# Second FFN: the order of high and low products inside a unit of matmuls, from "weights' low parts last" to triples

## The chip, the core and the metric

The kernel runs on one core of one Trainium2 chip. The metric is the device time of one execution in microseconds (us), as the median over runs; smaller is better.

## What is computed

One layer of a hybrid diffusion backbone on 256 latent tokens and 256 context tokens of width 2048, all in float32: a half-step SwiGLU FFN, a token mixer (grouped-query attention beside a two-way mLSTM), a second half-step FFN on the latent tokens alone, and a final norm. The change touches the second FFN:

```python
def half_step_ffn(x, mod, i, g, w_up, w_down):
    h = adaln(x, g, mod, i)
    a, b = jnp.split(h @ w_up, 2, axis=-1)
    return x + 0.5 * mod[:, i + 2, None, :] * ((jax.nn.silu(a) * b) @ w_down)
...
    xl = half_step_ffn(xl, mod_l, 6, g_norm[l, 2], w_ffn2_up[l], w_ffn2_down[l])
return rms_norm(xl, g_final)
```

Here `x` is 256 x 2048, `w_up` 2048 x 11264 and `w_down` 5632 x 2048.

## The kernel before

**A product in three matmuls.** Each float32 operand is split in two parts that TensorE takes in its faster float32 form: a high part `hi` and the rest `lo`. A product is then high x high, low x high and high x low. The tokens' parts (`h2hi`, `h2lo`, the forms `n1f`, `s4f`, `s2f`, and the hidden values `hid2h`, `hid2l`) stay in SBUF and are the stationary operand (128 x 128); the weights are the moving one (128 x 512). In the names of the profile `mm<-hi,hid2h` is a matmul with the weights' high part moving and the hidden values' high part stationary; `mm<-lo,hid2h` has the weights' low part moving.

**A unit.** Weights arrive as tiles of 128 x 2048 (1 MB). `split` (line 116) makes two halves of 1024 columns from a tile: for each half ScalarE (ACT) writes `hi` (line 124), then VectorE (DVE) writes `lo` as tile minus `hi` (line 125). There are four buffers of `hi` and four of `lo`, which is two tiles' worth. The matmuls on one tile are a unit. `products_in_order` (line 150) lays a unit out: first, for every product, high x high and tokens' low x weights' high; at the unit's end all products of the weights' low part. `issue` (line 165) emits them.

**The second FFN** has 11 groups of 512 hidden columns. Groups 2 to 10 run as a `quad` (line 2092), which forms the group's up products (256 tokens x 2048 x 1024) from seven block products instead of eight. Its seven steps (a11, a12, n1, s4, s2, s3, a22; lines 2150 to 2158) have two units each, called q0 and q1 here, with 12 matmuls to a unit, and gather in the PSUM banks `X` and `Y`. Sums of weight tiles that the scheme needs are made in place: on the tiles `chain2c` and `chain2r` by DMAs that add while they land (`accum`, line 751, issued by GpSimd, POOL), and once per quad by VectorE (in step n1, 128 x 2048, line 2094). Three steps give such DMAs, two each, as soon as both halves of the tile are split: a11 (they are read in n1), s4 and s2 (those of s2 are read in a22). The other weights come by plain DMAs on SyncE's queue (SP).

**Down products** of earlier groups are woven in between: `block` (line 2196) is a unit of 24 matmuls, for two token halves t = 0, 1 with a PSUM bank each. In quads after the first there is one block behind each of the steps a12, n1, s2 and s3 (line 2280). `down_pair` (line 2219) gathers two groups in PSUM before VectorE adds the bank of each t to `acc2` (`acc<-acc,mm`, line 2233). Group 1's up products (`up`, line 2172, 24 matmuls a unit) are woven into the first quad. After the last quad `down` (line 2238) adds the gate and, by DMA, the residual (line 1048 is the gate's product), and `last2` (line 2297) ends with the norm.

**Order.** The kernel emits instructions in the order of these loops; a scheduler in the language then sets the order on each engine, and may move an instruction whose operand comes late, by its own estimate. At run time each engine goes through its list in that order and stands at the first one that waits.

Of the kernel before, what the change touches and what calls it, by code (L numbers as in the profile page):

```python
# [41 lines left out]
FB = 4  # L42
CB = 512
# [11 lines left out]
def tile_layer(ctx: ExitStack, tc: tile.TileContext, I: dict, out: bass.AP):  # L55
# [7 lines left out]
    ps = {"mm": banks.enter_context(pool(name="ps", bufs=6, space=PSUM)), "tr": banks.enter_context(pool(name="pt", bufs=2, space=PSUM))}  # L63
# [86 lines left out]
    def products_in_order(ps, weights_still=False):  # L150

        early, late = [], []
        for o, sh, sl, mh, ml, first, last in ps:
            early.append((o, sh, mh, first, False))
            if weights_still:
                early.append((o, sh, ml, False, False))
                late.append((o, sl, mh, False, last))
            else:  # L160
                early.append((o, sl, mh, False, False))
                late.append((o, sh, ml, False, last))
        return early + late

    def issue(ms, skip=False):
        for o, st_, mv, first, last in ms:
            tensor[0].matmul(o, st_, mv, start=first, stop=last, skip_group_check=skip)  # L167
# [1107 lines left out]
    with ExitStack() as mx:  # L1275
# [586 lines left out]
        for cb in range(NCB):  # L1862
            bs = []
# [86 lines left out]
    with f2x:  # L1950
# [141 lines left out]
        def quad(n):  # L2092

            add = lambda o, x, y: nc.vector.tensor_tensor(o, x, y, op=ALU.add)
            mul = lambda o, x, y: nc.vector.tensor_tensor(o, x, y, op=ALU.mult)
            B, g = {}, {}
            chain_, ra = sets[n % 2], sets[1 - n % 2]

            def p1():
                g["a"] = ca_tile()  # L2100
                nc.scalar.activation(g["a"], B["X"], AF.Copy)

            def c11():
                add(g["a"], B["Y"], g["a"])
                nc.scalar.activation(g["a"], g["a"], AF.Silu)

            def kept():
                g["y"] = f2b.tile([P, CB], F32, tag="cy", name="cy", bufs=1)
                nc.scalar.activation(g["y"], B["Y"], AF.Copy)

            def p35():
                g["b"] = ca_tile()
                nc.scalar.activation(g["b"], B["Y"], AF.Copy)

            def c12():
                add(g["b"], B["X"], g["b"])
                mul(g["a"], g["a"], g["b"])
                turn.append((clock[0] + 2, n, 0, g["a"], -1.0))

            def c22():  # L2120
                assert (n, 0) in done
                add(g["y"], B["X"], g["y"])
                g["a"] = ca_tile()
                nc.scalar.activation(g["a"], B["X"], AF.Copy)

            def c21():
                add(g["a"], B["Y"], g["a"])
                nc.scalar.activation(g["a"], g["a"], AF.Silu)
                mul(g["a"], g["a"], g["y"])
                turn.append((clock[0] + 4, n, 1, g["a"], -1.0))  # L2130

            def chained(ab, c):
                return lambda q: accum(chain_[q], part(n, ab, c + q))

            def next_first(q):
                if n + 1 in QUADS:
                    nc.sync.dma_start(ra[q], part(n + 1, 0, q))

            def next_third(q):
                if n + 1 in QUADS:  # L2140
                    nc.sync.dma_start(chain_[q], part(n + 1, 1, 2 + q))

            def plain(q):
                r = raw_tile()
                nc.sync.dma_start(r, part(n, 0, 2 + q))
                return r

            held = lambda q: chain_[q]
            third = lambda q: ra[q]
            order = (  # L2150
                (a11, held, "X", True, chained(1, 0), p1),
                (a12, plain, "Y", True, None, c11),
                (n1, held, "Y", True, lambda q: add(chain_[q], chain_[q], ra[q]), kept),
                (s4, third, "Y", False, lambda q: accum(ra[q], part(n, 1, q)), p35),
                (s2, held, "X", False, chained(0, 2), c12),
                (s3, third, "X", False, next_first, c22),
                (a22, held, "Y", True, next_third, c21),
            )
            for m, (a, src, dst, fresh, then, use) in enumerate(order):
                for q in range(2):  # L2160
                    if q == 0 and fresh:
                        B[dst] = psx.tile([P, 512], F32, tag=dst, name=dst)
                    wt = split(src(q))
                    if then:
                        then(q)
                    ks = [(j, 4 * q + j) for j in range(4)]
                    issue(products_in_order([(B[dst], a[0][:, k, :], a[1][:, k, :], *wt(slice(j * CB, (j + 1) * CB)), fresh and k == 0, k == 7) for j, k in ks]), True)
                    if q:
                        use()
                    yield  # L2170

        def up(n):

            sab = []
            for ab in range(2):
                bs = [bank() for _ in range(2)]
                for u in range(4):
                    wt = load_split(part(n, ab, u))
                    ps = []
                    for j in range(4):  # L2180
                        k = 4 * u + j
                        for t in range(2):
                            tt = slice(t * P, (t + 1) * P)
                            ps.append((bs[t], h2hi[:, k, tt], h2lo[:, k, tt], *wt(slice(j * CB, (j + 1) * CB)), k == 0, k == KT - 1))
                    issue(products_in_order(ps))
                    if u == 3:
                        for t in range(2):
                            if ab:
                                nc.vector.tensor_tensor(sab[t], sab[t], bs[t], op=ALU.mult)
                                turn.append((clock[0] + 2, n, t, sab[t], 1.0))  # L2190
                            else:
                                sab.append(acc2[:, t, :CB])
                                nc.scalar.activation(sab[t], bs[t], AF.Silu)
                    yield

        def block(n, wt, ts=(0, 1), bs=None, first=True, last=True):

            bs = bs or [bank() for _ in ts]
            ps = []
            for j in range(FB):  # L2200
                for t, b in zip(ts, bs):
                    tt = slice(t * P, (t + 1) * P)
                    ps.append((b, hids[n][0][:, j, tt], hids[n][1][:, j, tt], *wt(slice(j * CB, (j + 1) * CB)), first and j == 0, last and j == FB - 1))
            issue(products_in_order(ps))
            return bs

        late = {}
# [241 lines left out]
```

## Time and profile before

| | |
|---|---|
| median of 3 runs | 2619.69 us (2619.2 to 2623.19) |
| the profiled execution | 2623.62 us, of which the span from first to last instruction is 2621.9 us |
| granted TensorE clock | 0.996 |
| TensorE busy | 2577.2 us (98%) |
| VectorE busy | 2167.5 us (83%) |
| ScalarE busy | 1420.9 us (54%) |
| second FFN's quads and what follows | from about 1953 us to the end |

Times in the views are in us from the start of the span. In a timeline a row has start, duration, engine, line, operation, output<-inputs, and how many instructions it merges; in square brackets is the idle time of the engine before it and what ended it. The ends of matmuls are modelled: they are issued every 0.227 us, while a row gives one 0.39 us, so the last 0.16 us of each lies beside the next. A group row gives busy time and mean ns, then idle time before.

### The profile page before, as it was taken

How to read it: one execution, taken by the hardware profiler on the slowest of the kernel's cores; microseconds unless marked ns; L12 is line 12 of the kernel's file. 1: busy time of each engine (PE TensorE's matmuls, PEld its weight loads, DVE VectorE, ACT ScalarE, POOL GpSimd, SP SyncE). 2: the span in 40 equal slices, each digit the busy share in tenths (PEclk: the TensorE clock that was granted, in tenths of full speed). 3: DMA queues.
4: the chain of work that ended last, by engine and by line, in shares of the span. 5: the costliest groups of instructions: out<-in, count | busy, mean ns of one | idle time of the engine just before them, and what ended most of it. 6: DMA issues, size and time to landing. Idle time of an engine off the chain costs nothing. (4 is left out here: it accounts for less than half of the span.)

```text
span 2621.9 us, 34118 instructions
## 1 busy us (share of the span) xinstructions
PE 2577.2 (98%) x12646; PEld 2139.4 (82%) x12646; DVE 2167.5 (83%) x2842; ACT 1420.9 (54%) x1876; POOL 216.4 (8%) x271
## 2 busy tenths in 40 slices
PE   8999999999999999999999999999999999999998
PEld 5788888888888888888889889888898877777776
DVE  7788888878888788888787889788898888888888
ACT  5454444454444465444454467567576656666664
POOL 0000010100010100000110000110000000000001
PEclk9999999999999999999999999999999999999999
DMA  9989999999999988889976877677678889998996
GB/s 401 350 210 269 277 270 284 256 272 285 275 268 284 263 242 235 226 218 231 228 233 261 306 275 246 230 262 277 235 277 236 253 249 259 261 263 259 262 266 192
DMA packets 127654, 684.71 MB, mean 261 GB/s; under 512 B 14200, under 2 KB 16760, under 8 KB 64896
## 3 DMA queue, kind: packets, MB, share of 16 engines
q1 hardware_dynamic: 98112, 490.63, 49.9%
q0 software_dynamic: 29376, 191.90, 37.1%
q8 instruction: 99, 1.62, 0.2%
q14 instruction: 67, 0.55, 0.1%
HBM read 664.59 MB, written 17.89 MB: 260 GB/s over the span
## 5 line engine op out<-in xcount | busy, mean ns | idle before, releaser
L125 DVE TENSOR_TENSOR lo<-raw,hi 128x1024 fp32r<-128x1024 f32 (+2 forms) x476 | 561.9, 1205 | 152.6 <-ACT hi L124 107.3
L124 ACT ACTIVATE hi<-raw 128x1024 fp32r<-128x1024 f32 (+2 forms) x488 | 492.1, 1036 | 345.0 <-PE mm L167 214.7
L167 PE MATMUL mm<-hi,hhi 128*128 128x512 f32 (+3 forms) x1024 | 392.1, 385 | 0.0
L167 PE MATMUL mm<-hi,hlo 128*128 128x512 f32 (+3 forms) x1024 | 386.0, 379 | 0.0
L124 ACT ACTIVATE hi<-chain 128x1024 fp32r<-128x1024 f32 x240 | 247.1, 1055 | 222.7 <-PE mm L167 109.4
L125 DVE TENSOR_TENSOR lo<-chain,hi 128x1024 fp32r<-128x1024 f32 x240 | 288.0, 1221 | 88.2 <-ACT hi L124 80.4
L167 PE MATMUL mm<-lo,hhi 128*128 128x512 f32 (+3 forms) x1024 | 253.4, 378 | 0.0
L228 DVE SCALAR_TENSOR_TENSOR junk<-sraw,cBh 128x1024 fp8e5<-128x1024 f32 x192 | 234.5, 1221 | 15.5 <-DMA sraw<-in_w_mt 13.3
L167 PEld LDWEIGHTS mm<-hi,hhi 128*128 128x128 f32 x1024 | 193.5, 189 | 31.5
L167 PEld LDWEIGHTS mm<-hi,hlo 128*128 128x128 f32 x1024 | 193.5, 189 | 31.1
L167 PEld LDWEIGHTS mm<-lo,hhi 128*128 128x128 f32 x1024 | 187.0, 188 | 33.1
L125 DVE TENSOR_TENSOR lo<-chain2c,hi 128x1024 fp32r<-128x1024 f32 x112 | 133.9, 1222 | 48.0 <-ACT hi L124 39.8
L125 DVE TENSOR_TENSOR lo<-chain2r,hi 128x1024 fp32r<-128x1024 f32 x104 | 124.1, 1222 | 48.1 <-ACT hi L124 40.4
L124 ACT ACTIVATE hi<-chain2c 128x1024 fp32r<-128x1024 f32 x112 | 113.0, 1052 | 87.8 <-DMA chain2c<-in_w_up2b 51.2
L124 ACT ACTIVATE hi<-chain2r 128x1024 fp32r<-128x1024 f32 x104 | 104.9, 1052 | 84.9 <-DMA chain2r<-in_w_up2b 37.1
L167 PE MATMUL mm<-hi,hid2h 128*128 128x512 f32 x352 | 137.2, 390 | 0.0
L167 PE MATMUL mm<-hi,hid2l 128*128 128x512 f32 x352 | 137.1, 390 | 0.0
L228 DVE SCALAR_TENSOR_TENSOR sr<-sr,cBl 128x1024 f32<-128x1024 f32 x85 | 102.7, 1218 | 14.8 <-DMA sr<-in_w_mt 14.7
L751 POOL DMA_DIRECT2D chain<-in_w_up1b x60 | 53.0, 884 | 728.0 <-DVE lo L125 700.7
L167 PE MATMUL mm<-lo,hid2h 128*128 128x512 f32 x352 | 87.6, 389 | 0.0
L167 PE MATMUL mm<-hhi,hi 128*128 128x512 f32 (+1 forms) x256 | 83.7, 346 | 0.0
L167 PE MATMUL mm<-hlo,hi 128*128 128x512 f32 (+1 forms) x256 | 81.2, 336 | 0.0
(512 smaller groups left out, 5609.0 us busy)
## 6 DMA issues: line engine op xcount, KB each, us to landing
raw<-in_w_dn SPq DMA_DIRECT2D x70, 1024.0 KB, 10.5
chain<-in_w_up1b POOLq DMA_DIRECT2D x60, 1024.0 KB, 9.8
sraw<-in_w_mt SPq DMA_DIRECT2D x96, 512.0 KB, 7.8
sr<-in_w_mt SPq DMA_DIRECT2D x82, 512.0 KB, 5.6
raw<-in_w_up1b SPq DMA_DIRECT2D x40, 1024.0 KB, 7.7
mraw<-in_w_m SPq DMA_DIRECT2D x32, 1024.0 KB, 7.7
chain<-in_w_dn POOLq DMA_DIRECT2D x30, 1024.0 KB, 9.3
chain2c<-in_w_up2b POOLq DMA_DIRECT2D x28, 1024.0 KB, 12.2
```

The source lines that it names most:

```text
L124: scalar[0].activation(hi, src, AF.Copy)
L125: vector[0].tensor_tensor(lo, src, hi.bitcast(F32), op=ALU.subtract)
L167: tensor[0].matmul(o, st_, mv, start=first, stop=last, skip_group_check=skip)
L228: ins = nc.vector.scalar_tensor_tensor(junk() if junk else raw, raw, 1.0, cB[s], op0=ALU.mult, op1=ALU.mult, accum_out=mT[:, i, s, kt, h : ...
L751: accum = lambda dst, src: nc.gpsimd.dma_start(dst, src, accum_op=ALU.add)
```

## The change

All units of the second FFN's quads, of `up` and of `block` are laid out in triples: for each product in turn high x high, high x weights' low, tokens' low x high. So the second matmul of a unit reads the weights' low part of the first half. In `block` the loop over token halves is now the outer one, so that t = 0's bank is complete after the first half of the unit. The first FFN and the mixer are as before. Three lines are new above, so later lines have numbers three higher.

```diff
+    def products_by_triple(ps):
+        return [m for o, sh, sl, mh, ml, first, last in ps for m in ((o, sh, mh, first, False), (o, sh, ml, False, False), (o, sl, mh, False, last))]
...
-                    issue(products_in_order([(B[dst], a[0][:, k, :], a[1][:, k, :], *wt(slice(j * CB, (j + 1) * CB)), fresh and k == 0, k == 7) for j, k in ks]), True)
+                    issue(products_by_triple([(B[dst], a[0][:, k, :], a[1][:, k, :], *wt(slice(j * CB, (j + 1) * CB)), fresh and k == 0, k == 7) for j, k in ks]), True)
...
-                    issue(products_in_order(ps))
+                    issue(products_by_triple(ps))
...
-            for j in range(FB):
-                for t, b in zip(ts, bs):
+            for t, b in zip(ts, bs):
+                for j in range(FB):
...
-            issue(products_in_order(ps))
+            issue(products_by_triple(ps))
```

The number of instructions is the same on every engine, and the orders on POOL and SP are the same. On TensorE the block behind step n1, in a quad of the middle of the second FFN, stood so before (its last high products and its low ones; `hi_17056` and `lo_17057` belong to the first half of the tile, `hi_17060` and `lo_17061` to the second, and `mm_17052`, `mm_17053` are the banks of t = 0 and 1):

```order
L167 MATMUL mm_17053<-hi_17060,hid2h_16591 128x512
L167 MATMUL mm_17053<-hi_17060,hid2l_16592 128x512
L167 MATMUL mm_17052<-lo_17057,hid2h_16591 128x512
L167 MATMUL mm_17053<-lo_17057,hid2h_16591 128x512
L167 MATMUL mm_17052<-lo_17057,hid2h_16591 128x512
L167 MATMUL mm_17053<-lo_17057,hid2h_16591 128x512
L167 MATMUL mm_17052<-lo_17061,hid2h_16591 128x512
```

The sixteen high products came first, and the second half's low part was read by the 21st matmul of the unit.

Now such a block begins as follows (`hi_18484`, `lo_18485` are the first half, `hi_18488`, `lo_18489` the second):

```order
L170 MATMUL mm_18480<-hi_18484,hid2h_17212 128x512
L170 MATMUL mm_18480<-lo_18485,hid2h_17212 128x512
L170 MATMUL mm_18480<-hi_18484,hid2l_17213 128x512
L170 MATMUL mm_18480<-hi_18484,hid2h_17212 128x512
L170 MATMUL mm_18480<-lo_18485,hid2h_17212 128x512
L170 MATMUL mm_18480<-hi_18484,hid2l_17213 128x512
L170 MATMUL mm_18480<-hi_18488,hid2h_17212 128x512
L170 MATMUL mm_18481<-hi_18484,hid2h_17212 128x512
L170 MATMUL mm_18481<-lo_18485,hid2h_17212 128x512
L170 MATMUL mm_18481<-hi_18484,hid2l_17213 128x512
L170 MATMUL mm_18481<-hi_18484,hid2h_17212 128x512
L170 MATMUL mm_18480<-lo_18489,hid2h_17212 128x512
```

The second matmul reads the first half's low part, and the scheduler has put four matmuls of t = 1 ahead of the first that reads the second half's low part: it is the 12th here, and the 8th in the units of the quads and nearly all other blocks.

On VectorE, around step n1 of such a quad (`chain2c` holds n1's two tiles, `raw` is the tile of the block behind it), the order before was:

```order
L125 TENSOR_TENSOR lo<-chain2c_16106,hi 128x1024
L2094 TENSOR_TENSOR chain2c_16106<-chain2c_16106,chain2r_16108 128x2048
L125 TENSOR_TENSOR lo<-chain2c_16107,hi 128x1024
L2233 TENSOR_TENSOR acc_16105<-acc_16105,mm 128x512 x2
L125 TENSOR_TENSOR lo<-chain2c_16107,hi 128x1024
L125 TENSOR_TENSOR lo<-raw,hi 128x1024
L2094 TENSOR_TENSOR chain2c_16107<-chain2c_16107,chain2r_16109 128x2048
L125 TENSOR_TENSOR lo<-raw,hi 128x1024
L125 TENSOR_TENSOR lo<-chain2r_16108,hi 128x1024 x2
```

and it is now:

```order
L125 TENSOR_TENSOR lo<-chain2c_16106,hi 128x1024
L2236 TENSOR_TENSOR acc_16105<-acc_16105,mm 128x512
L2097 TENSOR_TENSOR chain2c_16106<-chain2c_16106,chain2r_16108 128x2048
L2236 TENSOR_TENSOR acc_16105<-acc_16105,mm 128x512
L125 TENSOR_TENSOR lo<-chain2c_16107,hi 128x1024 x2
L125 TENSOR_TENSOR lo<-raw,hi 128x1024
L2097 TENSOR_TENSOR chain2c_16107<-chain2c_16107,chain2r_16109 128x2048
L125 TENSOR_TENSOR lo<-raw,hi 128x1024
L125 TENSOR_TENSOR lo<-chain2r_16108,hi 128x1024 x2
```

Both additions to `acc2` of the block before n1 have moved from between the two splits of n1's q1 tile to ahead of them.

Around step a22, before (`chain2r` holds a22's tiles):

```order
L125 TENSOR_TENSOR lo<-chain2r_16108,hi 128x1024
L125 TENSOR_TENSOR lo<-chain2r_16109,hi 128x1024
L2233 TENSOR_TENSOR acc_16105<-acc_16105,mm 128x512 x2
L125 TENSOR_TENSOR lo<-chain2r_16109,hi 128x1024
L125 TENSOR_TENSOR lo<-chain2c_16106,hi 128x1024 x2
```

and now:

```order
L125 TENSOR_TENSOR lo<-chain2r_16108,hi 128x1024
L2236 TENSOR_TENSOR acc_16105<-acc_16105,mm 128x512
L125 TENSOR_TENSOR lo<-chain2r_16109,hi 128x1024
L2236 TENSOR_TENSOR acc_16105<-acc_16105,mm 128x512
L125 TENSOR_TENSOR lo<-chain2r_16109,hi 128x1024
L125 TENSOR_TENSOR lo<-chain2c_16106,hi 128x1024 x2
```

One of the two additions has moved ahead of the first split of a22's q1 tile; the other still stands between the two.

## Prediction

> **What bounds the kernel now.** The page first: TensorE is busy nearly all the time.
>
> ```profile
> PE 2577.2 (98%) x12646; PEld 2139.4 (82%) x12646; DVE 2167.5 (83%) x2842; ACT 1420.9 (54%) x1876; POOL 216.4 (8%) x271
> ```
>
> An average can hide a stage, so next the stretches of 200 us (core time, then PE, PEld, DVE, ACT, POOL busy, granted clock, DMA share, GB/s), one from the first FFN and one from the second.
>
> ```profile
> 400.00:600.00 200.00, 200.00 (x901) 165.49 (x900) 159.12 (x201) 94.02 (x112) 19.41 (x22) 1.00 0.97 270
> 2200.00:2400.00 200.00, 191.48 (x843) 154.93 (x843) 165.68 (x155) 123.10 (x136) 15.67 (x18) 1.00 0.88 253
> ```
>
> The first FFN leaves TensorE no gap. The second does, at full clock, so something else paces it. Its quads repeat; three stretches cut at the ends of a22 show how long one takes.
>
> ```profile
> 2111.23:2177.25 66.02, 62.15 (x273) 49.91 (x272) 53.22 (x51) 39.76 (x45) 5.22 (x6) 1.00 0.88 255
> ...
> 2499.73:2561.49 61.76, 61.35 (x274) 50.20 (x272) 53.19 (x51) 39.77 (x45) 5.23 (x6) 1.00 0.87 241
> 2111.23:2561.49 450.26, 432.61 (x1906) 350.04 (x1904) 372.57 (x351) 278.92 (x309) 36.57 (x42) 1.00 0.89 257
> ```
>
> Seven quads take 450.26 us: 66.02 for the first, 61.76 for the last, and (450.26 - 66.02 - 61.76) / 5 = 64.50 for each of the five between. The last has no next quad to fetch for, and TensorE is busy in 61.35 of its 61.76 us. So TensorE's own work is at most 61.4 us a quad and the other five have about 3 us more. What are they waits for? The list of TensorE's waits in the second FFN (us in total, times, longest):
>
> ```profile
> PE Y L167 <- DVE lo L125: 12.5, 14, 1.0
> PE Y L167 <- ACT hi L124: 7.2, 8, 1.4
> ```
>
> TensorE waits only at units of `Y`, for splits: the places are q1 of n1 and q1 of a22, whose tiles come by adding DMAs. ScalarE's timeline has the starts of the splits when such tiles have landed (a22, n1, the next a22), and POOL's has the first adding DMA that is given after each.
>
> ```profile
> 2236.42 2.01 ACT L124 ACTIVATE hi<-chain2r 128x1024 fp32r<-128x1024 f32 x2 [3.89 <-PE Y L167]
> ...
> 2259.84 2.01 ACT L124 ACTIVATE hi<-chain2c 128x1024 fp32r<-128x1024 f32 x2 [3.22 <-DMA chain2c<-in_w_up2b]
> ...
> 2300.75 2.01 ACT L124 ACTIVATE hi<-chain2c 128x1024 fp32r<-128x1024 f32 x2 [3.91 <-PE Y L167]
> ```
>
> ```profile
> 2243.74 0.86 POOL L751 DMA_DIRECT2D chain2c<-in_w_up2b  x1 [27.88 <-DVE lo L125]
> ...
> 2271.64 0.88 POOL L751 DMA_DIRECT2D chain2r<-in_w_up2b  x1 [24.18 <-DVE lo L125]
> ```
>
> This is a loop: landing for a22 at 2236.42, 7.32 us until POOL gives the next DMA, 16.10 until the tile for n1 is in, 11.80 until the next DMA, 29.11 until a22's tile. Together 64.33: the quad's length. DMAs take 45.2 us of it, and the reaction to a landing, on ScalarE and VectorE, 19.1. VectorE's timeline at n1 shows what the 11.80 consist of:
>
> ```profile
> 2260.93 1.23 DVE L125 TENSOR_TENSOR lo<-chain2c,hi 128x1024 fp32r<-128x1024 f32 x1 [1.52 <-ACT hi L124]
> 2262.08 1.28 DVE L2233 TENSOR_TENSOR acc<-acc,mm 128x512 f32<-128x512 f32 x2
> 2263.27 1.22 DVE L125 TENSOR_TENSOR lo<-chain2c,hi 128x1024 fp32r<-128x1024 f32 x1
> 2264.41 1.22 DVE L125 TENSOR_TENSOR lo<-raw,hi 128x1024 fp32r<-128x1024 f32 x1
> 2265.54 2.29 DVE L2094 TENSOR_TENSOR chain2c<-chain2c,chain2r 128x2048 f32<-128x2048 f32 x1
> 2267.74 1.22 DVE L125 TENSOR_TENSOR lo<-raw,hi 128x1024 fp32r<-128x1024 f32 x1
> 2268.88 4.63 DVE L125 TENSOR_TENSOR lo<-chain2r,hi 128x1024 fp32r<-128x1024 f32 x4
> ```
>
> VectorE runs without a gap from 2260.93: split, two additions to `acc2`, split, split, weight sum, split, then s4's two splits, after which POOL can give s4's DMA.
>
> **The change, part by part.** *The matmuls themselves.* Same number, same form. TensorE's rows at n1:
>
> ```profile
> 2261.28 1.98 PE L167 MATMUL Y<-hi,n1f 128*128 128x512 f32 x8
> 2263.09 0.61 PE L167 MATMUL Y<-lo,n1f 128*128 128x512 f32 x2
> 2264.55 0.73 PE L167 MATMUL Y<-lo,n1f 128*128 128x512 f32 x2 [0.84 <-DVE lo L125]
> 2265.12 0.39 PE L167 MATMUL mm<-hi,hid2h 128*128 128x512 f32 x1
> ...
> 2270.57 1.98 PE L167 MATMUL Y<-hi,s4f 128*128 128x512 f32 x8
> ```
>
> Eight take 1.81 us, 0.227 each, and the block of 24 from 2265.12 to 2270.57 takes 5.45, high or low alike. New order within a bank: 0.
>
> *VectorE's order at n1.* Both additions move ahead of the tile's first split. Before it VectorE stands idle for 1.52 us, and the block that they add ended before n1, so there they cost nothing; behind it they took 2263.27 - 2262.08 = 1.19. The reaction becomes 11.80 - 1.19 = 10.61. If that cover were gone they would cost 1.19 again.
>
> *VectorE's order at a22.*
>
> ```profile
> 2237.50 1.23 DVE L125 TENSOR_TENSOR lo<-chain2r,hi 128x1024 fp32r<-128x1024 f32 x1 [4.48 <-ACT hi L124]
> 2238.65 1.28 DVE L2233 TENSOR_TENSOR acc<-acc,mm 128x512 f32<-128x512 f32 x2
> ```
>
> One of the two additions leaves the way: half of 1.19, 0.60 (here 4.48 us idle cover it).
>
> Whether 0.60 reaches the landing depends on the DMAs' load (last but one column):
>
> ```profile
> 2266.00:2268.00 2.00, 2.00 (x10) 1.65 (x10) 2.00 (x2) 0.99 (x2) 0.00 (x0) 1.00 0.00 0
> 2268.00:2270.00 2.00, 2.00 (x11) 1.65 (x10) 2.00 (x2) 1.15 (x2) 0.00 (x0) 1.00 0.10 16
> ...
> 2301.00:2308.00 7.00, 5.30 (x22) 3.85 (x22) 6.16 (x7) 6.41 (x7) 0.00 (x0) 1.00 0.97 377
> 2308.00:2317.00 9.00, 9.00 (x44) 7.42 (x43) 9.00 (x10) 6.69 (x10) 1.76 (x2) 1.00 0.99 229
> ```
>
> During the reaction at n1 the DMAs stand still, so 1.19 us less of it is 1.19 us less of quad. At a22 they are full (0.97, 0.99) with plain loads, and an earlier adding DMA only takes its share from those. Of the 0.60 I count 0.2, between 0 and 0.6. So a paced quad goes from 64.50 to 63.1 (-1.4), with 62.7 and 63.3 as ends. The Trainium skill, "DMA: Bandwidth & Descriptors", section "Issuing engines are not separate DMA queues", says that transfers from all issuing engines run on the same 16 DMA engines and interleave. By that rule alone the 0.60 would bring nothing, and a quad would take 63.3; the rows 0.97 and 0.99 agree.
>
> *TensorE's new waits.* It now needs the first half's low part at its second matmul. From n1's landing (2259.84 = 0), with 1.14 a split (2263.27 to 2264.41) and 2.20 for the sum (2265.54 to 2267.74): low parts of q1 at 2.2 and 3.4, of the block at 4.5 and 7.8. TensorE starts q1 at 1.44, goes on at 2.3, and 11 matmuls later has finished at 4.8; before at 5.28. The block's 12th matmul is due at 4.8 + 11 x 0.227 = 7.3 and waits until 7.9: 0.6. The block ends at 10.85, before at 10.73. At a22 q1 it has 2.2 us to wait for the low part after the landing instead of 1.1, but the second half is there 0.6 earlier: 0 to +0.4. Added to 61.4, TensorE's own quad is at most 62.4, below 63.1, so these waits lie in time in which it would wait for a tile anyway. Where no DMA paces, they show: I count 0.5 for each of the first two quads, 1.0 in all (0 to 3), and -0.3 for the last quad, whose n1 and a22 lose an addition's wait (0 to -0.6).
>
> *Buffers.* The first half's high part is free after 6 matmuls instead of 4, the second after 12 instead of 8: 0.45 and 0.9 us later. At s4 that gives its second high part 4.8 + 0.2 + 0.6 (a copy from `Y` now stands ahead of it on ScalarE) + 0.95 (half of the 2.01 rows) after the landing, 6.6; VectorE comes to it at about 9. Covered: 0.
>
> *The end.* VectorE's rows after the last block's weights have come:
>
> ```profile
> 2593.09 1.28 DVE L2246 TENSOR_TENSOR acc<-acc,mm 128x512 f32<-128x512 f32 x2
> 2594.29 1.29 DVE L1048 SCALAR_TENSOR_TENSOR acc<-acc,g 128x512 f32<-128x512 f32 x2
> 2595.49 3.49 DVE L125 TENSOR_TENSOR lo<-raw,hi 128x1024 fp32r<-128x1024 f32 x3
> ```
>
> Four instructions stand between two splits there; in the new order one addition of the four comes earlier, into VectorE's idle time: -0.6 (0 to -1.5).
>
> Sum: +1.0, six paced quads x -1.4 = -8.4, -0.3, -0.6: **-8.3 us**. The profiled execution took 2623.62, of which 2621.9 is span; it would take 2615.3. It lies 3.9 above the median of 2619.69, and I take the same difference from that: **2611.4**.
>
> **The rivals.**
>
> *More: TensorE alone paces.* If the accumulating DMAs also run faster because plain loads fall later, a quad comes down to TensorE's own 61.4 to 62.4, say 62.0: 6 x -2.5 - 0.9 + 1.0 = -14.9, 2604.8. For it: DMA share 0.89 leaves the DMAs some 7 us idle in a quad. Against: the 29.11 us stage has been full.
>
> *No change: the DMAs give nothing back.* The landing for a22 comes when four adding DMAs and the plain loads are through; if the plain loads take the 1.19 us, the quads stay at 64.5 and only +1.0 - 0.3 - 0.6 is left: 2619.8. For it: the shares of 0.97 and 0.99; against: 0.00 and 0.10 in the reaction.
>
> *Slower: the low part's wait is not hidden.* At both landings of a quad TensorE stands before its second matmul until VectorE's split is done, 1.1 us later than now, and holds everything behind it; finishing a unit after that takes 11 matmuls where now 2 or 4 are left. If VectorE does not come to the splits earlier (because the additions, now ahead of them in its order, wait for the block's second bank) each landing costs 0.7 and the block 0.6: 2.0 a quad, 7 x 2.0 + 1.0 = +15, 2634.7. It decides when the block before n1 ends so late that the second addition, 0.6 us, and a split, 1.14, are not done within n1 q0's 12 matmuls, 2.72 us: a margin of 0.9 now. The first FFN's down products already go in triples at 200.00 of 200.00 busy, which speaks against it. The Trainium skill, "TensorE: Matmul & The Clock Gate", Part 2, says that matmuls stay in program order and only weight loads are pulled ahead. By it a late low part stops the whole queue, which is this rival; the trace agrees, as the 0.84 above stopped the block behind it.
>
> **How the numbers follow.** A measurement of this kernel tells about 0.2%, 5.2 us, from no change. Forecast 0.45, more 0.12, no change 0.25, slower 0.18. Of the forecast's 0.45 a part (terms at their weak ends) falls inside 5.2 us: faster 0.53, same 0.29, slower 0.18. The range takes in the first three with their ends and the lighter part of the slower case: 2603 to 2626.
>
> **What would show it.** Right: quads of 63.1 in the cut stretches; first adding DMA 10.6 after n1's landing and 6.7 after a22's; TensorE's waits moved from n1 and a22 to the block behind n1, some 0.6 each. Wrong: quads still at 64.5 although the reaction is shorter (DMAs), or above it with longer waits for `lo` (slower), or additions on VectorE that wait for `mm` ahead of the splits.

## The result, and the profile after

The changed kernel takes 2609.86 us (median of 4 runs, 2605.14 to 2611.2), the kernel before beside it 2621.07 (4 runs, 2619.2 to 2623.19): a ratio of 0.9953, with a 95% interval of 0.9937 to 0.9969. That is 11.2 us less; 8.3 were forecast. The profiled execution took 2609.54 us, of which the span is 2607.8.

The page's line of engines hardly moved, TensorE's 2577.2 us became 2575.1:

```profile
PE 2575.1 (99%) x12646; PEld 2138.1 (82%) x12646; DVE 2172.8 (83%) x2842; ACT 1435.6 (55%) x1876; POOL 216.3 (8%) x271
```

The stretches cut at the ends of a22 show the quads: first, third, fourth and fifth, then all seven in one (columns as in the prediction).

```profile
2108.39:2171.16 62.77, 62.02 (x274) 50.04 (x272) 53.78 (x51) 41.37 (x44) 5.22 (x6) 1.00 0.93 269
...
2234.66:2300.56 65.90, 62.56 (x274) 50.02 (x272) 53.80 (x51) 41.13 (x44) 5.21 (x6) 1.00 0.89 255
2300.56:2362.34 61.78, 61.49 (x274) 50.19 (x272) 54.63 (x51) 41.74 (x44) 5.21 (x6) 1.00 0.92 265
2362.34:2423.81 61.47, 61.15 (x273) 50.20 (x272) 53.86 (x51) 41.57 (x44) 5.24 (x6) 1.00 0.92 273
...
2108.39:2548.71 440.32, 432.62 (x1906) 350.84 (x1905) 377.89 (x352) 290.24 (x308) 36.55 (x42) 1.00 0.91 265
```

Seven quads take 440.32 us where they took 450.26: 62.90 each on average, not 64.32. They are no longer alike: some run at 61.5 with TensorE busy nearly throughout, one takes 65.90. Between the two spans (2621.9 and 2607.8, 14.1 apart) the seven quads account for 9.9, the time up to the first cut (2111.23 and 2108.39) for 2.8, and the rest behind the last for 1.3.

TensorE's waits in the second FFN (us in total, times, longest) fell from 12.5 and 7.2 to:

```profile
PE Y L170 <- DVE lo L125: 3.6, 6, 0.8
PE Y L170 <- ACT hi L124: 1.9, 3, 1.1
PE mm L170 <- DVE lo L125: 1.7, 6, 0.3
```

The wait at `mm` is new, six times. The two reactions of the loop are read as before: ScalarE's splits of the tiles for a22, n1 and the next a22, which have just landed, and POOL's first adding DMA behind each.

```profile
2229.27 2.01 ACT L124 ACTIVATE hi<-chain2r 128x1024 fp32r<-128x1024 f32 x2 [3.84 <-DMA chain2r<-in_w_up2b]
...
2254.34 2.00 ACT L124 ACTIVATE hi<-chain2c 128x1024 fp32r<-128x1024 f32 x2 [3.81 <-DMA chain2c<-in_w_up2b]
...
2295.20 2.01 ACT L124 ACTIVATE hi<-chain2c 128x1024 fp32r<-128x1024 f32 x2 [3.97 <-DMA chain2c<-in_w_up2b]
```

```profile
2236.00 0.86 POOL L754 DMA_DIRECT2D chain2c<-in_w_up2b  x1 [26.97 <-DVE lo L125]
...
2264.93 0.88 POOL L754 DMA_DIRECT2D chain2r<-in_w_up2b  x1 [25.20 <-DVE lo L125]
...
2301.92 0.88 POOL L754 DMA_DIRECT2D chain2r<-in_w_up2b  x1 [26.81 <-DVE lo L125]
```

So 6.73 us at a22 (2229.27 to 2236.00), 18.34 until n1's tile is in, 10.59 at n1 (2254.34 to 2264.93), and 30.27 for the four DMAs. The reactions were 7.32 and 11.80. These rows are from the slowest of the seven quads: its stage of 18.34 stands out, the other six took 15.3 to 17.0 there. VectorE's timeline at this n1 shows the difference:

```profile
2253.71 0.68 DVE L2236 TENSOR_TENSOR acc<-acc,mm 128x512 f32<-128x512 f32 x1
2255.42 2.36 DVE L125 TENSOR_TENSOR lo<-chain2c,hi 128x1024 fp32r<-128x1024 f32 x2 [1.03 <-ACT hi L124]
2257.70 1.22 DVE L125 TENSOR_TENSOR lo<-raw,hi 128x1024 fp32r<-128x1024 f32 x1
2258.84 2.28 DVE L2097 TENSOR_TENSOR chain2c<-chain2c,chain2r 128x2048 f32<-128x2048 f32 x1
2261.04 1.22 DVE L125 TENSOR_TENSOR lo<-raw,hi 128x1024 fp32r<-128x1024 f32 x1
2262.17 2.35 DVE L125 TENSOR_TENSOR lo<-chain2r,hi 128x1024 fp32r<-128x1024 f32 x2
```

Both additions are through before VectorE's idle 1.03 us ends, and from there to s4's second split nothing is left but splits and the weight sum.

### The profile page after: what moved, and what is told of

Read it like the earlier page. It is cut to its first block, busy times and chain, and to the rows that moved or that the text cites. A ratio compares the mean times of both kernels' runs of the same rounds, so it can differ in the third digit from the quotient of the medians.

```text
span 2607.8 us, 33942 instructions
## 1 busy us (share of the span) xinstructions
PE 2575.1 (99%) x12646; PEld 2138.1 (82%) x12646; DVE 2172.8 (83%) x2842; ACT 1435.6 (55%) x1876; POOL 216.3 (8%) x271
## 4 chain that ended last, share of the span: by engine, by line
PE 78%; DMA 10%; DVE 6%; issue 3%; ACT 1%; POOL 0%; SPq 0%; POOLq 0%; ACTq 0%; DVEq 0%
PE mm L170 48%; PE mm L147 4%; PE mm L148 4%; PE mm L146 4%; DMA chain2c<-in_w_up2b 4%; PE Y L170 4%; DMA chain2r<-in_w_up2b 3%; DVE lo L125 3%; PE X L170 2%; PE mm L83 2%; PE tr L147 2%; PE tr L148 2%; PE tr L146 2%; DMA mraw<-in_w_m 1%; ACT hi L124 1%
## 5 line engine op out<-in xcount | busy, mean ns | idle before, releaser
L124 ACT ACTIVATE hi<-raw 128x1024 fp32r<-128x1024 f32 (+2 forms) x488 | 497.7, 1038 | 358.5 <-PE mm L170 208.7
L170 PE MATMUL mm<-lo,hid2h 128*128 128x512 f32 x352 | 137.8, 392 | 1.7 <-DVE lo L125 1.7
L170 PEld LDWEIGHTS mm<-lo,hid2h 128*128 128x128 f32 x352 | 66.1, 188 | 18.4 <-DVE lo L125 5.0
```

Source lines behind the costliest of these rows:

```text
L124: scalar[0].activation(hi, src, AF.Copy)
```

## Experiments

**The theory**: the gain is the 1.19 us (n1) and 0.60 us (a22) that two VectorE additions no longer take between a landing and the next adding DMA. **Rival one**: TensorE gains from the triples. **Rival two**: buffers freed later spread the plain loads, so the adding DMAs land sooner. The table holds every run. The reactions are from the start of ScalarE's split to POOL's next adding DMA, as above; where engine order alone sets them they repeat to 0.02 us from quad to quad. In late_add_pin, late_sum_pin and late_sum_pb the split at a22 starts when TensorE frees a buffer, in nearly every quad, and the tile has landed before that. The quads are the seven, from one profiled execution each. The ratio is to the kernel before, timed on the same chip.

| kernel | at n1 | at a22 | quads, mean | median | ratio (95%) |
|---|---|---|---|---|---|
| before | 11.80 | 7.32 | 64.32 | 2621.07 | |
| before, again | 11.80 | 7.32 | 64.00 | 2616.07 (one run) | |
| the whole change | 10.61 | 6.73 | 62.90 | 2609.86 | 0.9953 (0.9937-0.9969) |
| block_only | 10.61 | 6.73 | 63.80 | 2612.69 | 0.9961 (0.9947-0.9974) |
| quads_only | 11.80 | 7.33 | 64.43 | 2618.15 | 0.9993 (0.9977-1.0008) |
| per_bank | 10.61 | 6.73 | 62.65 | 2610.07 | 0.9952 (0.9935-0.9969) |
| late_add_pin | 11.93 | 7.3-7.6 | 65.22 | 2623.5 | 1.0009 (0.9996-1.0021) |
| j_outer | 10.61 | 7.33 | 62.74 | 2610.04 | 0.9971 (0.9961-0.9982) |
| moved_block | 8.33 | 6.73 | 62.23 | 2606.18 | 0.9953 (0.9937-0.9968) |
| half_block_loads | 10.7-11.7 | 6.73 | 62.03 | 2605.64 | 0.9946 (0.9932-0.9960) |
| half_accum | | | 65.34 | 2630.18 | 1.0045 (1.0032-1.0059) |
| late_sum_pin | 8.7-9.9 | 6.8 | 60.83 | 2595.25 | 0.9911 (0.9898-0.9923) |
| late_sum_pb | 8.4-8.8 | 6.7-7.2 | 60.90 | 2591.72 | 0.9905 (0.9892-0.9918) |
| late_sum_b | 9.60 | 7.33 | 60.96 | 2598.05 | 0.9924 (0.9908-0.9939) |

### Which part of the change

**The down blocks alone** (`block` as in the change, `quad` and `up` as before):

```diff
-                    issue(products_by_triple([(B[dst], a[0][:, k, :], ...
+                    issue(products_in_order([(B[dst], a[0][:, k, :], ...
...
-                    issue(products_by_triple(ps))
+                    issue(products_in_order(ps))
```

> Only the down blocks are in the new order (token halves outside, triples); the quads' own units and group 1's up units keep the low parts last. VectorE's additions then stand where the whole change put them: both ahead of n1's q1 splits, one of two ahead of a22's. Theory (the additions leave the reaction to a landing, and nothing else matters): first adding DMA 10.6 us after n1's landing and 6.7 after a22's, quads of 62.9 on average as in the whole change, 2610 us (2607 to 2613). Rival one (the gain is TensorE's, from the triples in the quads' units): no gain, 2620. Rival two (buffers freed later spread the plain loads, so the adding DMAs land sooner): the blocks are a quarter of the units, so a quarter to a half of the gain, 2615 to 2618.

```profile
2108.70:2555.31 446.61, 433.94 (x1905) 349.15 (x1904) 375.40 (x351) 278.83 (x309) 36.63 (x42) 1.00 0.91 261
```

The reactions are those of the whole change, and so is the time within the intervals. The quads of this one execution, the slowest of the kernel's eleven, are longer than expected, 63.80; "before, again" below shows how much an execution adds by itself.

**The quads' units alone** (`block` as before, the rest as in the change):

```diff
-            for t, b in zip(ts, bs):
-                for j in range(FB):
+            for j in range(FB):
+                for t, b in zip(ts, bs):
...
-            issue(products_by_triple(ps))
+            issue(products_in_order(ps))
```

> The quads' units and group 1's up units are in triples; the down blocks are as before, so the two additions stand between n1's q1 splits again. Theory: reactions of 11.8 and 7.3 us as before, quads of 64.3 to 65, since the triples can only add waits for the low part (up to 0.5 a quad): 2620 to 2624 us. Rival one (triples in the quads): the whole gain, 2610. Rival two (later buffers): half to three quarters of it, 2612 to 2616.

```profile
2107.91:2558.91 451.00, 434.99 (x1906) 350.37 (x1905) 374.27 (x350) 288.55 (x308) 36.63 (x42) 1.00 0.89 257
```

No gain: 451.00 for seven quads, ratio 0.9993 with 1 in its interval. Rival one falls, and rival two with it, since these units are three quarters of all.

**No triples at all**, in the kernel before: each bank's products by themselves, its low parts last.

```diff
-            ps = []
-            for j in range(FB):
-                for t, b in zip(ts, bs):
+            for t, b in zip(ts, bs):
+                ps = []
+                for j in range(FB):
                     tt = slice(t * P, (t + 1) * P)
...
-            issue(products_in_order(ps))
+                issue(products_in_order(ps))
```

> No triples at all: the down blocks run one token half after the other, each with its low parts last, all else as before. The first half's bank is complete after 12 matmuls, and both additions stand ahead of n1's q1 splits. Theory: it is the exchange of the loops that frees the additions, not the triples: 10.6 and 6.7 us, quads of 62.9, 2610 us (2607 to 2613). Rival one (triples): 2620. Rival two (buffers): the first half's high part is freed after 18 of 24 matmuls instead of 14, so some of the gain, 2615.

```profile
2108.80:2547.36 438.56, 430.24 (x1906) 350.81 (x1904) 374.33 (x350) 280.55 (x309) 36.64 (x42) 1.00 0.92 265
```

The whole gain without a single triple: the exchange of the loops suffices to bring the additions ahead of n1's splits.

**The whole change with the additions put back behind the splits:**

```diff
-                            for t in range(2):
-                                a = acc2[:, t, cb * CB : (cb + 1) * CB]
-                                nc.vector.tensor_tensor(a, a, bs[cb][t], op=ALU.add)
+                            owed.append((cb, bs[cb]))
...
+                    if q:
+                        pay()
                     ks = [(j, 4 * q + j) for j in range(4)]
```

`pay` emits the owed additions and keeps them in that place.

> The whole change, but the down pairs' additions are emitted behind the splits of the next q1 unit and kept there, so that both stand in the reaction at n1 and both at a22; TensorE's order and the buffers stay those of the whole change. Theory: 11.8 us after n1's landing and 7.9 after a22's (two additions there, before it was two less one), quads of 64.4 to 65, the whole gain gone: 2619 to 2624 us. Rivals one and two (TensorE's order, or the buffers and loads): 2610, as the whole change.

VectorE after n1's landing at 2254.28:

```profile
2255.38 2.36 DVE L125 TENSOR_TENSOR lo<-chain2c,hi 128x1024 fp32r<-128x1024 f32 x2 [1.46 <-ACT hi L124]
2257.77 2.29 DVE L2097 TENSOR_TENSOR chain2c<-chain2c,chain2r 128x2048 f32<-128x2048 f32 x1
2259.98 1.28 DVE L2232 TENSOR_TENSOR acc<-acc,mm 128x512 f32<-128x512 f32 x2
2261.18 2.35 DVE L125 TENSOR_TENSOR lo<-raw,hi 128x1024 fp32r<-128x1024 f32 x2
2263.45 2.35 DVE L125 TENSOR_TENSOR lo<-chain2r,hi 128x1024 fp32r<-128x1024 f32 x2
```

```profile
2107.68:2564.19 456.51, 438.78 (x1906) 355.91 (x1905) 378.71 (x352) 292.51 (x308) 36.63 (x42) 0.99 0.89 255
```

Both additions stand in the way again, the quads take 65.22 on average, and the whole gain is gone (1.0009) although TensorE's units are still in triples. But this run does not test the loop, because its time goes another way. The block's low parts come after the additions here too, and TensorE waits for them in every quad, 10.3 us more than in the kernel after:

```profile
PE mm L170 <- DVE lo L125: 12.0, 7, 1.8
```

In four of the seven quads the granted clock (last column but two) then falls to 0.50, as here:

```profile
2262.45 0.70 PE L170 MATMUL mm<-lo,hid2h 128*128 128x512 f32 x1 [1.61 <-DVE lo L125]
```

```profile
2262.00:2264.00 2.00, 1.55 (x4) 1.26 (x5) 2.00 (x3) 0.00 (x0) 0.00 (x0) 0.65 0.00 0
2264.00:2266.00 2.00, 2.00 (x6) 1.51 (x6) 1.80 (x2) 0.00 (x0) 0.00 (x0) 0.50 0.65 188
```

The block's remaining 22 matmuls take 6.9 us in such a quad and 5.3 in another: 4 x 1.6 = 6.4 us. The two, 10.3 and 6.4, account for the 16.2 by which these seven quads (456.51) are longer than those after (440.32). And a22's tile no longer paces: its split starts behind TensorE in all seven, as in this row, with the tile in.

```profile
2230.68 1.06 ACT L124 ACTIVATE hi<-chain2r 128x1024 fp32r<-128x1024 f32 x1 [1.93 <-PE mm L170]
```

So the case for the two additions rests on the others: the gain is there in block_only, in per_bank and in j_outer (next), where they stand ahead of n1's splits, and not in quads_only, where they stand between. That the loop is how they cost time is shown by late_sum_b, further down.

**The 0.60 at a22.** The loops of `block` in the old order, all in triples: both additions stand ahead of n1's splits, and behind the first split at a22.

```diff
-            for t, b in zip(ts, bs):
-                for j in range(FB):
+            for j in range(FB):
+                for t, b in zip(ts, bs):
```

> The whole change without the exchange of the loops in the down blocks: triples, but the two token halves in turn for each product, so that both banks are complete only at the block's end. On VectorE both additions stand ahead of n1's q1 splits all the same, while at a22 both stand behind the first split, as before. Theory: 10.6 us after n1's landing and 7.3 after a22's, so the 1.19 is gained and the 0.60 isn't; of the 0.60 I counted 0.2 a quad: 7 x 0.2 = 1.4 us more than the whole change, 2611 us (2609 to 2615). Rival (the exchange of the loops is what the gain hangs on): 2620.

```profile
2118.48:2557.68 439.20, 431.88 (x1906) 350.76 (x1905) 375.34 (x350) 289.60 (x308) 36.57 (x42) 1.00 0.91 263
```

Quads of 62.74, against 62.90 with the 0.60 gained: nothing to be seen of it. The ratio, 0.9971, is a little behind the whole change, but the intervals overlap. A term of 0.2 a quad is below what this study can tell, so it stays open between 0 and 0.4. The prediction took from the Trainium skill, "DMA: Bandwidth & Descriptors", section "Issuing engines are not separate DMA queues", that transfers of all issuing engines share the same 16 DMA engines, and concluded that the 0.60 would bring nothing; these quads are in line with that and do not prove it.

The rival falls: the gain does not hang on the exchange of the loops. Triples in the block, or the exchange (per_bank), each bring the additions ahead of n1's splits. Why the scheduler places them there was not looked into.

### How much is one execution's

**The kernel before, profiled again:**

> The kernel before, unedited, profiled once more, to see how much of a difference between two profiles is the execution's. Theory: reactions of 11.80 and 7.33 us to the hundredth, since they are engine time; stages of the adding DMAs up to 1 us apart from the first profile, quads of 64.3 on average. If the first quad again ends near 2111, the 2.8 us that the whole change gained there are the change's; if it ends near 2108, they were that one execution's.

```profile
2169.34:2233.24 63.90, 61.73 (x274) 50.03 (x273) 53.27 (x51) 40.02 (x45) 5.23 (x6) 1.00 0.91 266
2233.24:2299.17 65.93, 62.13 (x273) 49.87 (x272) 53.37 (x51) 40.02 (x45) 5.22 (x6) 1.00 0.88 256
...
2106.88:2554.85 447.97, 433.38 (x1906) 351.08 (x1904) 373.18 (x352) 279.90 (x309) 36.57 (x42) 1.00 0.90 259
```

The reactions repeat to 0.02 us. The first cut is at 2106.88, so the 2.8 us at the start were one execution's and not the change's; and quads from 62 to 66 occur before as well as after. Two profiles of the same kernel differ by 2.3 us in the seven quads (450.26 and 447.97).

### What else the loop holds

**The block behind n1 moved behind s4**, so that its two splits leave the reaction too:

```diff
-... else {1: 1, 2: 1, 4: 1, 5: 1}
+... else {1: 1, 3: 1, 4: 1, 5: 1}
```

> The whole change, and in quads after the first the down block behind n1 goes behind s4, so its two splits (2 x 1.14 us) leave the reaction to n1's landing. Theory: 8.3 us there instead of 10.6, 6.7 at a22 as before; the loop would then take 60.6, less than TensorE's own 61.2 to 61.5, so TensorE paces: quads of 61.5, 2609.9 less 7 x 1.4 = 2600 us (2598 to 2605). Rival (DMAs at 0.91 of their time are the bound, and what the reaction gives back they take): quads stay near 62.9, 2610. If a new wait at s4 (its tile is now needed directly behind n1) takes it back: 2610 to 2615.

```profile
2110.39:2546.02 435.63, 430.03 (x1906) 351.15 (x1905) 378.06 (x351) 292.67 (x308) 36.57 (x42) 1.00 0.91 267
```

```profile
PE Y L170 <- ACT cy L2112: 5.5, 8, 0.7
```

The reaction is 8.33 as computed, and the landings no longer hold TensorE up. But ScalarE's copy of `Y` after n1 was hidden behind that block, and s4 now waits 0.7 for it in each quad: 62.23, and a ratio no better than that of the whole change. The third case of the expectation, in part.

**Half of the down pairs' weights left out:**

```diff
-                        wt = load_split(I["w_dn2"][m, cb])
+                        raw = raw_tile()
+                        nc.sync.dma_start(raw[:, :1024], I["w_dn2"][m, cb][:, :1024])
+                        wt = split(raw, same=True)
```

> The whole change, but the down pairs' weight tiles are loaded by half and both halves are split from that one, which leaves out half of these weights: 2 of some 16.7 MB a quad; all instructions on the engines stay. Theory (adding DMAs share the 16 DMA engines with the plain loads, and with reactions of 10.6 and 6.7 the loop still ends last in some quads): DMA share from 0.91 to about 0.81, stages of adding DMAs 2 to 4 us shorter together, quads at TensorE's own 61.3, 2600 us (2598 to 2605). Rival (adding DMAs take their own time whatever is beside them): quads of 62.9, 2610.

```profile
2107.30:2541.54 434.24, 431.34 (x1905) 351.00 (x1904) 375.68 (x351) 291.44 (x308) 36.55 (x42) 1.00 0.85 233
```

Between theory and rival. The DMA share falls from 0.91 to 0.85, and the stage from a22's first adding DMA to n1's landing from 16.6 to 15.1 us (means of the seven), while that of the four DMAs stays at 28 to 30. Fewer bytes beside them help the adding DMAs, but only where those bytes lie: 1.5 us for the three block tiles there, 1.5 MB less.

**Adding DMAs in halves:**

```diff
-                return lambda q: accum(chain_[q], part(n, ab, c + q))
+                return lambda q: halves(chain_[q], part(n, ab, c + q))
+            def halves(x, src):
+                for h in range(2):
+                    accum(x[:, h * 1024 : (h + 1) * 1024], src[:, h * 1024 : (h + 1) * 1024])
```

> The whole change, but each adding DMA of the second FFN's quads is given as two of half the columns, the first as soon as the first half is split. Theory: the first adding DMA goes out 1.14 us earlier at both landings (9.5 and 5.6); if the DMAs' stages keep their length from the first issue on, the loop loses 2.3 a quad and TensorE paces at 61.5: 2600 us. Rival (a DMA has a fixed part besides its bytes, doubled here, and POOL needs 0.87 to give each): stages longer by as much or more, 2610 to 2625.

The last landings of such a stage, on ScalarE (two halves of one tile):

```profile
2230.36 1.06 ACT L124 ACTIVATE hi<-chain2r 128x1024 fp32r<-128x1024 f32 x1 [3.15 <-DMA chain2r<-in_w_up2b]
2235.39 1.06 ACT L124 ACTIVATE hi<-chain2r 128x1024 fp32r<-128x1024 f32 x1 [3.96 <-DMA chain2r<-in_w_up2b]
```

The rival holds: slower, 1.0045. Two halves land 5.03 us apart; two whole tiles, in the kernel after, 7.52 apart (splits at 2287.68 and 2295.20):

```profile
2287.68 2.01 ACT L124 ACTIVATE hi<-chain2c 128x1024 fp32r<-128x1024 f32 x2 [1.49 <-DMA chain2c<-in_w_up2b]
```

From 5.03 for half the bytes and 7.52 for all follows a part of some 2.5 us that does not depend on bytes, here as an estimate under this load. The Trainium skill, "DMA: Bandwidth & Descriptors", section "Anatomy of one DMA — SWDGE (gpsimd) path", gives about 2.0 us as the fixed part of one DMA; these rows are near it. A half goes in as many packets as a whole (144), so the rows can't tell a cost of the DMA from one of its packets. Nor is all of the loss the DMAs': TensorE waits up to 2.4 us for these tiles, and six times the granted clock then falls to about 0.50.

**n1's second weight sum later.** Only the second adding DMA and step s2 need it, but it stood ahead of the first:

```diff
+            def summed1(q):
+                if not q:
+                    add(chain_[0], chain_[0], ra[0])
+            def summed2(q):
+                accum(ra[q], part(n, 1, q))
+                if not q:
+                    pin(add(chain_[1], chain_[1], ra[1]))
...
-                (n1, held, "Y", True, lambda q: add(chain_[q], chain_[q], ra[q]), kept),
-                (s4, third, "Y", False, lambda q: accum(ra[q], part(n, 1, q)), p35),
+                (n1, held, "Y", True, summed1, kept),
+                (s4, third, "Y", False, summed2, p35),
```

> The whole change, and the second of n1's two weight sums on VectorE (2.2 us, needed by the second adding DMA after n1 and by step s2, not by the first adding DMA) goes behind s4's first two splits and is kept there. Block, DMAs and TensorE's units stay where they are, and so does the work that covers the copy from Y. Theory: first adding DMA 8.4 us after n1's landing instead of 10.6; the loop then takes 60.8, so TensorE paces: quads of 61.2 to 61.5, 2609.9 less 7 x 1.5 = 2599 us (2597 to 2604). Rival (the adding DMAs take back what the reaction gives): quads of 62.9, 2610.

VectorE at n1 (landing at 2250.26) and the first and last quad:

```profile
2255.91 1.22 DVE L125 TENSOR_TENSOR lo<-chain2r,hi 128x1024 fp32r<-128x1024 f32 x1
2257.64 1.23 DVE L125 TENSOR_TENSOR lo<-chain2r,hi 128x1024 fp32r<-128x1024 f32 x1 [0.52 <-ACT hi L124]
2258.78 2.28 DVE L2097 TENSOR_TENSOR chain2c<-chain2c,chain2r 128x2048 f32<-128x2048 f32 x1
```

```profile
2111.94:2172.77 60.83, 60.83 (x273) 50.35 (x272) 54.27 (x51) 41.83 (x44) 5.23 (x6) 1.00 0.95 277
2476.93:2537.76 60.83, 60.83 (x274) 50.35 (x272) 54.19 (x51) 42.10 (x44) 5.23 (x6) 1.00 0.90 247
```

Every quad takes 60.83 us, TensorE is busy in all of it, and its list of waits is empty from there to the end of the quads. The sum now lies behind s4's splits, POOL's DMA goes out 8.7 to 9.9 after the landing (where it is over 8.4, s4's buffers are what it waits for), and the time is 2595.25, ahead of both kernels by more than their intervals.

The same on the version without triples (per_bank):

> The same late weight sum on the version without triples, whose blocks run one token half after the other with the low parts last. There the block behind n1 waited for its second low part, which came behind the sum (TensorE's waits for mm, 6.4 us in 7 quads). Theory: 8.4 us after n1's landing, that wait gone too, quads of 61.2 to 61.5 and 2599 us (2597 to 2604), no different from the late sum with triples. Rival (low parts in triples matter once TensorE paces): one of the two versions is faster by over 3 us.

```profile
2104.84:2531.16 426.32, 426.24 (x1905) 352.16 (x1904) 376.59 (x351) 282.63 (x309) 36.55 (x42) 1.00 0.95 273
```

2591.72, the best median of the study. It is 3.5 us ahead of the version with triples, just over the rival's 3, but the intervals overlap, so whether triples matter here stays open. And on the kernel before, with nothing else:

> The kernel before with the late weight sum alone: its products in their old order, its additions between n1's q1 splits. Theory: first adding DMA 9.6 us after n1's landing and 7.3 after a22's; with 16.4 and 29.1 for the adding DMAs' stages the loop takes 62.4, still more than TensorE's own 60.8, so quads of 62 to 62.5 and 2619 less 7 x 2 = 2605 us (2601 to 2608): the change tried here and the late sum add up until TensorE paces. Rival (the late sum alone already reaches TensorE's own pace, so that the change under study is then worth nothing): quads of 60.8, 2595 us.

```profile
2108.16:2534.86 426.70, 426.19 (x1906) 352.11 (x1904) 373.71 (x351) 284.23 (x309) 36.56 (x42) 1.00 0.94 272
```

Here the theory's number fell. The reactions are 9.60 and 7.33 as expected, yet the quads take 60.96, not 62 to 62.5. The step that failed was to keep 29.1 us for the four adding DMAs: counted from the first of them to the split of a22's tile, they now take 27.6 to 28.4. A reading that fits, not tested by itself: the first goes out 4.5 us ahead of the second, where it was 2.3, and lands 8.0 us later (8.1 in the kernel before), so it is over halfway through when the others come. So the late sum alone reaches TensorE's pace, and with it the change studied here has nothing left to gain that these runs can tell: 0.9924 (0.9908 to 0.9939) without it, 0.9911 and 0.9905 with.

This run also settles a rival that was not named: the additions hold n1's second low part back, and TensorE's wait for it (0.84 us in the prediction's rows) might have been the whole cost, without any loop. Here they still stand between the two splits:

```profile
2248.73 1.28 DVE L2242 TENSOR_TENSOR acc<-acc,mm 128x512 f32<-128x512 f32 x2
2249.92 1.22 DVE L125 TENSOR_TENSOR lo<-chain2c,hi 128x1024 fp32r<-128x1024 f32 x1
```

Yet of 22 waits at `Y`, 19.7 us in all, one is left:

```profile
PE Y L167 <- DVE lo L125: 0.5, 1, 0.5
```

With the reaction 2.2 us shorter the tiles land early enough for TensorE not to notice the additions.

## Why the prediction was right

**What paces.** The loop of landings and reactions was the right reading. Reactions of 10.61 and 6.73 were forecast as 10.6 and 6.7, and shortening the one at n1 by other means leads to quads that TensorE alone paces, from the kernel before (late_sum_b) as from the one after (late_sum_pin).

**Quads.** Forecast 63.1 for a paced quad and -8.7 us for all; measured 62.90 on average, -9.9 between the two profiles first compared, -7.7 against the second profile of before. The -1.4 a quad was right within that scatter, but as a mean: the picture of five equal quads was one execution's. In the kernel after, some quads run at TensorE's pace, and others wait on a stage of adding DMAs, which takes 27.4 to 30.4 us. Counted over six loops, from the first adding DMA behind a22 on POOL to the same place six quads later, a loop takes 64.75 us before (2113.28 to 2501.78), 64.36 before again (2108.55 to 2494.70) and 63.21 after (2109.70 to 2488.95). Less the reactions (19.12, 19.12 and 17.34) that leaves 45.6, 45.2 and 45.9 for the DMAs: their stages became no shorter, against rival two and the rival "more", and longer by 0.3 to 0.7, not much above the 0.4 between the two of before. One profile can hide the gain altogether: in block_only's, with the same reactions, 47.0 is left and the loops take 64.37 (2108.88 to 2495.07); there only the medians show it.

**TensorE's own quad** was put at 61.4 at most, and up to 62.4 with the new waits. It is 60.83, with triples or without. Without that miss the rival "TensorE alone paces" would have been priced lower than 2604.8; it is where late_sum_pin went.

**The new waits.** At the block behind n1 0.6 was forecast; its 11th and 12th matmul:

```profile
2261.60 0.39 PE L170 MATMUL mm<-hi,hid2h 128*128 128x512 f32 x1
2262.31 0.50 PE L170 MATMUL mm<-lo,hid2h 128*128 128x512 f32 x1 [0.32 <-DVE lo L125]
```

It is the 12th that waits: 2262.31 - 2261.60 = 0.71, of which 0.227 is its turn, so 0.48. It cost nothing that quads_only or block_only can show, as forecast: the slower rival (2634.7) needed the additions to wait ahead of the splits, and VectorE had 1.03 us idle left there. late_add_pin, where VectorE does come late to the block's low parts, shows that such waits are dear. The "no change" rival falls too: the six loops above became 1.2 to 1.5 us shorter each, of 1.8 taken from the reactions.

**Start and end.** +1.0 was counted for the first quads; from the first matmul into `X` to the first cut it is 144.1 us after, 146.8 and 144.0 in the two profiles of before, so about 0 instead. The end was put at -0.6: what follows the last cut takes 59.1, before 60.4 and 59.5, so -0.4 to -1.3. Of the 2.9 us between the forecast of -8.3 and the -11.2 of the medians the start accounts for 1.0 and the end for 0.2; the interval of the ratio (-8.1 to -16.5 us) holds the rest.

## What to carry to other kernels

Where an engine with 98% busy time still waits, look for a loop through a queue of transfers: the time from a landing to the next transfer that depends on it is paid once per round, and an instruction standing in that stretch, however short, can be worth its full length (the 1.19 us at n1, where the DMAs stood still) or nothing that shows (the 0.60 at a22, where they were full), while a few rows earlier it costs nothing. List everything in the stretch and ask of each whether the next transfer needs it; here a new order of matmuls led a scheduler to move 1.2 us out, and a 2.2 us sum that nothing needed yet had been standing beside it. Before reading a microsecond out of two profiles, profile the same kernel twice. And when work is put back to test a cause, look for the wait that it opens elsewhere: late_add_pin gave back the right number of microseconds for another reason.

## What the runs showed of the hardware

Where engine order alone sets it, the time between two events repeats from one execution to the next to 0.02 us, while adding DMAs of equal size in equal places do not: 27.4 to 30.4 us for the stage of four. Even the start of the quads moves, behind a program that is the same up to the last few units; these are the first matmuls into `X` in late_sum_pb and j_outer:

```profile
1960.80 0.39 PE L167 MATMUL X<-hi,h2hi 128*128 128x512 f32 x1
```

```profile
1969.89 0.39 PE L170 MATMUL X<-hi,h2hi 128*128 128x512 f32 x1
```

That is 9 us, half of the spread between single runs of the kernel before (2609.34 to 2627.69 in one series). The granted clock is a part of it: in j_outer it was 0.59 from 40 to 44 us and 0.83 and 0.75 in the two stretches of 4 us from 1464 to 1472, and 1.00 there in late_sum_pb, by which some 3 us can be lost (an estimate, 4 x (0.41 + 0.17 + 0.25)). What makes the rest of it and the DMAs vary was not tried and stays open.

A wait of TensorE can cost more than its length. Behind waits of 1.61 to 1.80 us in late_add_pin, and of 1.97 in one quad of before_again, the granted clock fell to 0.50 for some 3 to 4 us and the matmuls came every 0.43 us instead of 0.227. It did not after every such wait (two of 1.80 in late_add_pin left it at 1.00), nor anywhere in the seven quads of the kernel after.
